# Stick-breaking attention on one core: two heads as one unit, each on its half of the array's rows, and softplus over a whole head

## The chip, the core and the metric

The kernel runs on one core of a Trainium2 chip. The metric is device time in microseconds, from the first to the last instruction of an execution and what lies around it, lower being better. Most executions of a kernel agree within 0.3%.

## What is computed

The kernel is two transformer blocks on 512 tokens of width 1024 in float32. The first has a mixer of stick-breaking attention and a gated linear recurrence (called hgrn in the code), then a mixture of experts; the second has retention, differential attention, attention to a memory and a feed-forward part. The change lies in the stick-breaking attention of the first block: 8 heads of 64 dimensions, 512 queries and keys.

```python
z = einsum('bhqd,bhkd->bhqk', q_blk, k) * dh ** -0.5
mask = key_pos[None, :] < q_pos[:, None]
log_beta = log_sigmoid(z)
log_keep = where(mask, log_sigmoid(-z), 0.0)
later = concatenate([log_keep[..., 1:], zeros_like(log_keep[..., :1])], axis=-1)
log_survive = cumsum(later, axis=3, reverse=True)
a = where(mask, exp(log_beta + log_survive), 0.0)
out = einsum('bhqk,bhkd->bhqd', a, v)
```

With softplus(z) = max(z, 0) + log(1 + exp(-|z|)), log_sigmoid(z) is z - softplus(z) and log_sigmoid(-z) is -softplus(z). So a weight is exp(z minus the sum of softplus over this key and all later ones that the query sees).

## The kernel before

**Products.** A float32 product of the projections is made of three passes over operands split into a rounded part (hi) and the rest (lo): `mm3`, lines 187 to 189. Weights come by DMA in chunks of 128 x 1024 and are split by ScalarE (ACT, L169) and VectorE (DVE, L170). `ws` gives [columns, tokens] by column tiles of 128, 24 products of 512 columns for a tile when the depth is 1024; `ts` gives [tokens, columns]. Their results stand in PSUM under the tag "mm" (2 banks). Attention uses the tag "at" (4 banks) and, for results, "tp" (2 banks).

**Order of the work.** The program is written one operation after the other, and the Tile layer's planner turns it into one fixed order for each engine before the kernel runs: an instruction goes as early as the planner's model has its operands and buffers ready, and of several that are ready the one written first goes first. Work that is written later, such as the gate products behind the attention, thus fills in where the attention would leave an engine idle. Each engine then works in that order and waits on semaphores.

**Slots.** `slot` hands out 128 x 512 tiles of one pool, NSL = 21. The hgrn stage takes 20 of them, 4 of which come free with each of its first three pairs of heads and 8 with the last. Behind them come, in the order of the program, 4 slots for values (`sv_`), 8 for queries (`sq_`), 4 for keys (`sk_`) and 11 of the 16 gates; the other five gates (GX) have a pool of their own, slp2.

**Queries, keys, values.** `ts` makes the values. Then, for each pair t of heads, `ws` makes the pair's queries and keys, 128 rows each, with head 0 on rows 0 to 63 and head 1 on rows 64 to 127. `ev_sq` (L572 to L580) evacuates the queries into a tile of their own for each head, the other head's 64 rows being zeroed by GpSimd (POOL, L578): a product with all 128 rows of the keys then gives that head's scores. The keys are copied as they are (L585).

**A head** (`sb_head`, L605 to L641). Keys lie on partitions. For key block j, only the queries from block j on matter, so that the four blocks have 512, 384, 256 and 128 columns, 1280 in all.

- Scores: for each block a float32 matmul of 128 rows (L615) and a bf16 matmul that adds the mask's -1e30 on the diagonal block (L616, identity times `negsb`). A float32 matmul stands in the profile as two records, its two passes.
- Softplus, block by block: DVE copies the scores to z (L617), ACT takes the absolute value, Exp and Ln (L619 to L621) in one of three buffers "ea", DVE adds max(z, 0) (L622), and `hilo` (L253 on ACT, L254 on DVE) splits the result into ph and pl.
- Sums over later keys: for each block j, products of the triangle or of ones with ph and pl of the blocks from j on (L633, L634), into a bank of "at".
- Weights and values: DVE subtracts the sums from z (L636), ACT takes Exp (L637), and a float32 matmul with 64 columns of the values (L638) writes the head's half of the partitions of y. `hilo` splits y at the end.

z, ph and pl have two buffers each, so a head's can be in use beside the next one's. The scores of the next head take the same four banks "at" as the sums of this one.

**Gates.** Two calls of `ws` behind the heads make 16 tiles; ACT copies each to its slot (L653). Their sigmoids wait for the last Exp of the attention. Then the branch products take the attention's result ysb.

Two other places have matmuls on a half of the array: hgrn's values (L557), where two heads write the two halves of the output partitions, one right behind the other, and differential attention's scores in block 2 (L1182), with 64 rows of each operand and a mask product between one and the next.

Of the kernel before, what the change touches and what calls it, by code (L numbers as in the profile page):

```python
# [8 lines left out]
F32 = mybir.dt.float32  # L9
# [11 lines left out]
S = 512  # L21
# [7 lines left out]
NSL = 21  # L29
GX = (5, 6, 7, 8, 9)  # L30
NRX = 8
NRX2 = 12
# [51 lines left out]
def body(tc, a, out):  # L84
# [106 lines left out]
    def ws(w2, nk, c0, ntile, x, n, evac, lead=0, raws=()):  # L191
        """[cols, tokens] = w2[:, c0:]^T x, by column tiles of 128; `lead` first tiles by halves of the tokens."""
        xh, xl = parts(x)
        per = CE // (nk * 128)
        got = []
        for j in range(ntile):
            if j % per == 0:
                if j // per < len(raws):
                    got = [split(None, nk, per * 128, raws[j // per])]
                else:  # L200
                    got = [load(w2, 0, nk, c0 + j * 128, min(per, ntile - j) * 128)]
            wh, wl = got[0]
            cc = slice((j % per) * 128, (j % per) * 128 + 128)
            if j < lead:
                if j == 0:
                    firsts = []
                o = psum("mm")
                firsts.append((o, wh, wl, cc))
                if j == lead - 1:
                    for hf in range(2):  # L210
                        t0, t1 = hf * n // 2, (hf + 1) * n // 2
                        for o, wh, wl, cc in firsts:
                            for k in range(nk):
                                mm3(o[:, t0:t1], wh[:, k, cc], wl[:, k, cc], xh[k][:, t0:t1], xl[k][:, t0:t1],
                                    k == 0, k == nk - 1)
                    for i, f in enumerate(firsts):
                        evac(i, f[0][:, :n])
                continue
            o = psum("mm")
            for k in range(nk):  # L220
                mm3(o[:, :n], wh[:, k, cc], wl[:, k, cc], xh[k][:, :n], xl[k][:, :n], k == 0, k == nk - 1)
            evac(j, o[:, :n])

    def ts(w2, nk, c0, ntok, x, evac, by_token=True, tag="mm", after=None, korder=None, new=None):
        """[tokens, 512 cols] = x^T w2[:, c0:c0+512]; one block of 128 tokens after the other or all along k."""
# [32 lines left out]
    def normed(xrow, g, p, pre=None):  # L258
        """rmsnorm of 128 rows; `pre`: mean square of the first half, and eps, already summed."""
# [35 lines left out]
    def rms_bcast(m, n, p, w=S, rbufs=2, name="rb"):  # L295
        """1/rms, from sums of squares that stand on every partition."""
        q = p.tile([128, S], F32, name=name, bufs=rbufs)[:, :w]
        A.activation(q, m, AF.Ln, bias=epsc, scale=1.0 / n)
        A.activation(q, q, AF.Exp, scale=-0.5)
        return q  # L300
# [8 lines left out]
    # =====================================================================  # L309
    # block 1, mixer  # L310
    # =====================================================================
# [36 lines left out]
    negsb = cp.tile([128, 128], BF, name="negsb")  # L348
# [17 lines left out]
    # lower bound: first row of the softmax over the two logits  # L366
# [13 lines left out]
    # weights of the differential attention's two maps, and its gains  # L380
# [66 lines left out]
    # cumulative log f inside blocks of 128 tokens; k = 1 - f  # L447
# [26 lines left out]
    def hgrn_pair(t):  # L474
# [43 lines left out]
        # between blocks of 128: the state behind each block, both heads on its diagonal  # L518
# [51 lines left out]
    # stick-breaking attention  # L570
    sq_, sk_, sv_ = {}, {}, {}

    def ev_sq(t0):
        def f(t, o):
            for h in range(2):
                q = slot("sq")
                sq_[2 * (t0 + t) + h] = q
                G.memset(q[64 - 64 * h:128 - 64 * h, :], 0.0)  # L578
                A.activation(q[64 * h:64 * h + 64, :], o[64 * h:64 * h + 64, :], AF.Copy, scale=0.125)
        return f  # L580
# [18 lines left out]
    slp2 = pool("slp2", 1, stack=at)  # L599
# [6 lines left out]
    def sb_head(h):  # L606
        t = h // 2
        z = sb.tile([128, 1280], F32, name="z", bufs=2)
        ph = sb.tile([128, 1280], F32R, name="ph", bufs=2)
        pl = sb.tile([128, 1280], F32R, name="pl", bufs=2)  # L610
        for j in range(4):
            n = S - 128 * j
            cc = slice(COL[j], COL[j + 1])
            o = psum("at")[:, :n]
            T.matmul(o, sk_[t][:, j * 128:(j + 1) * 128], sq_[h][:, j * 128:], start=True, stop=False)  # L615
            T.matmul(o[:, :128], identb, negsb, start=False, stop=True)  # L616
            V.tensor_copy(z[:, cc], o)  # L617
            e = sb.tile([128, S], F32, name="ea", bufs=3)[:, :n]
            A.activation(e, o, AF.Abs)  # L619
            A.activation(e, e, AF.Exp, scale=-1.0)  # L620
            A.activation(e, e, AF.Ln, bias=onec)  # L621
            V.scalar_tensor_tensor(e, z[:, cc], 0.0, e, op0=OP.max, op1=OP.add)  # L622
            hilo(ph[:, cc], pl[:, cc], e)
        y = psum("tp", name="ysbp")
        for j in range(4):
            n = S - 128 * j
            cc = slice(COL[j], COL[j + 1])
            o = psum("at")[:, :n]
            for i in range(j, 4):
                m = tri if i == j else onesr  # L630
                ci = slice(COL[i], COL[i + 1])
                oo = o[:, (i - j) * 128:]
                T.matmul(oo, m, ph[:, ci], start=(i == j), stop=False)  # L633
                T.matmul(oo, m, pl[:, ci], start=False, stop=(i == 3))  # L634
            w = sb.tile([128, S], F32, name="ea", bufs=3)[:, :n]
            V.tensor_sub(w, z[:, cc], o)  # L636
            last_exp[:] = [A.activation(w, w, AF.Exp)]  # L637
            T.matmul(y[64 * (h % 2):64 * (h % 2) + 64, 128 * j:], sv_[j][:, h * 64:(h + 1) * 64], w,  # L638
                     start=(j == 0), stop=(j == 3))
        p0 = 64 * (h % 2)  # L640
        hilo(ysb[0][p0:p0 + 64, t, :], ysb[1][p0:p0 + 64, t, :], y[p0:p0 + 64, :])  # L641

    for h in range(8):
        sb_head(h)

    # gates
    gt = {}

    def ev_gate(key):
        def f(t, o):  # L650
            n = t + (8 if key == "h" else 0)
            gt[key, t] = slot("gt") if n not in GX else slp2.tile([128, S], F32, name="gt2", bufs=len(GX))
# [7 lines left out]
    # branches, output product  # L660
# [40 lines left out]
    def residual_product(w2, xT, p, then, tag="at", korder=None):  # L701
        """x += xT^T w2, the second half of the columns by blocks of tokens; then(t, mean square of the first half)."""
# [13 lines left out]
    # memory rows for the keys and values, and the experts' weights  # L716
# [61 lines left out]
    # =====================================================================  # L778
    # block 1, mixture of experts
    # =====================================================================  # L780
# [6 lines left out]
    def place(v):  # L787
        """per entry of four, how many others stand before it from the greatest down, the earlier of equals first."""
# [32 lines left out]
    # place of a token among its expert's, -1 if it isn't one of them  # L821
# [3 lines left out]
    # weights of the choices  # L825
# [30 lines left out]
    # per token and expert: the token's place, 1, and its weight in three bf16 parts that add up to it  # L856
# [11 lines left out]
    def slots_of(pi, n, ix, w):  # L868
        """row numbers and weights of an expert's slots, from the products with its one-hots."""
# [21 lines left out]
    # experts with more than CAP tokens: how many further blocks  # L891
# [20 lines left out]
    # keys and values of the memory  # L912
# [24 lines left out]
    # rows and outputs of two experts; their transposed rows in both parts  # L937
    XG = hp.tile([128, 4, D], F32, name="XG", tag="hTh")
    XT = hp.tile([128, 4, 8, CAP], F32R, name="XT", tag="hTl")
    def fetch(ix, i):  # L940
        """rows of an expert's slots."""
# [3 lines left out]
    def prep(j, i):  # L945
        """fetched rows, transposed, in both parts."""
# [74 lines left out]
    def load_ahead(e):  # L1021
        """weights that stand ready behind the further blocks, as many as there are buffers."""
# [79 lines left out]
    # values of the memory, behind the experts  # L1102
# [23 lines left out]
    # =====================================================================  # L1126
    # block 2, retention and differential attention
    # =====================================================================
# [186 lines left out]
    # =====================================================================  # L1315
    # block 2, attention to the memory
    # =====================================================================
# [63 lines left out]
    # =====================================================================  # L1381
    # block 2, feed-forward
    # =====================================================================
# [61 lines left out]
```

## Time and profile before

| | |
|---|---|
| median of 3 runs | 1651.45 us |
| lowest to highest | 1650.45 to 1652.04 us |
| span of the profiled execution, first to last instruction | 1649.3 us |
| share of the span: TensorE, DVE, ACT, POOL busy | 98%, 59%, 51%, 5% |

The profiled execution has no time of its own beside its span. Its instructions are given by engine (PE is TensorE's matmuls, PEld its weight loads) and by the line of the code above. A matmul's recorded duration contains the way through the array, so that matmuls which follow each other overlap in the record: what one costs is the distance from its start to the next one's. In a timeline, equal neighbours are merged into one row with their number behind an x. In [ ] stands the idle time of the engine before an instruction and what ended it.

### The profile page before, as it was taken

To read this page: it belongs to the slowest core of one execution; us is meant where nothing else is said; L and a number is where in the kernel's file an instruction comes from. 1 tells how busy PE (TensorE), PEld (TensorE's weight loads), DVE (VectorE), ACT (ScalarE), POOL (GpSimd) and SP (SyncE) were. 2 spreads that over 40 slices of the span, in tenths; PEclk is the share of its full clock that TensorE was granted. 3 is DMA by queue.
4 is the path that set the end of the run, shared out by engine and by line. 5 is a ranking of instruction groups with operands and counts; after the bars stand their busy time and mean duration, and the time that the engine had idled before them with its cause. 6 is when DMAs were issued, how large, how long until landed. Compare 5 with 4: busy or idle time off the path is not lost. (4 is left out here: it accounts for less than half of the span.)

```text
span 1649.3 us, 20584 instructions
## 1 busy us (share of the span) xinstructions
PE 1610.5 (98%) x7695; PEld 1243.8 (75%) x7695; DVE 965.2 (59%) x1541; ACT 837.9 (51%) x1339; POOL 75.1 (5%) x92
## 2 busy tenths in 40 slices
PE   7999999999999999999999999999999999999999
PEld 6887776678878777776677667667878888888887
DVE  6459946544647999998755656455654433333221
ACT  5444556664346888888765545424443423232210
POOL 3000000000001211111110000000000000000000
PEclk9999999999999999999999999999999999999999
DMA  7230220133479999999944113123311333333231
GB/s 229 65 102 26 65 78 26 52 102 98 148 254 301 358 368 365 361 359 374 368 161 141 52 55 86 45 71 114 104 51 51 115 91 101 98 94 103 90 128 39
DMA packets 203071, 242.89 MB, mean 147 GB/s; under 512 B 10400, under 2 KB 133560, under 8 KB 202968
## 3 DMA queue, kind: packets, MB, share of 16 engines
q1 hardware_dynamic: 188800, 205.43, 37.3%
q0 software_dynamic: 7056, 24.27, 5.2%
q10 hardware_dynamic: 7112, 11.85, 2.3%
q8 instruction: 61, 1.00, 0.2%
q14 instruction: 42, 0.34, 0.1%
HBM read 223.69 MB, written 15.73 MB: 145 GB/s over the span
## 5 line engine op out<-in xcount | busy, mean ns | idle before, releaser
L170 DVE TENSOR_TENSOR wlo<-wraw,whi 128x1024 fp32r<-128x1024 f32 x210 | 256.0, 1223 | 280.0 <-ACT whi L169 269.8
L169 ACT CAST whi<-wraw 128x1024 fp32r<-128x1024 f32 x210 | 220.5, 1051 | 380.2 <-PE ps L188 259.8
L187 PE MATMUL ps<-hTh,whi 128*128 128x512 f32 (+1 forms) x912 | 349.7, 384 | 1.3 <-DVE fsg L1396 0.8
L188 PE MATMUL ps<-hTl,whi 128*128 128x512 f32 (+1 forms) x912 | 348.2, 382 | 0.9 <-DVE hTl L254 0.9
L189 PE MATMUL ps<-hTh,wlo 128*128 128x512 f32 (+1 forms) x912 | 347.6, 381 | 0.0
L170 DVE TENSOR_TENSOR wlo<-rx,whi 128x1024 fp32r<-128x1024 f32 x176 | 210.6, 1220 | 36.3 <-ACT whi L169 34.4
L169 ACT CAST whi<-rx 128x1024 fp32r<-128x1024 f32 x176 | 182.8, 1049 | 52.7 <-PE ps L189 30.2
L187 PEld LDWEIGHTS ps<-hTh,whi 128*128 128x128 f32 x912 | 172.1, 189 | 34.6 <-issue 1.8
L188 PEld LDWEIGHTS ps<-hTl,whi 128*128 128x128 f32 x912 | 172.1, 189 | 33.4 <-issue 1.8
L189 PEld LDWEIGHTS ps<-hTh,wlo 128*128 128x128 f32 x912 | 172.1, 189 | 31.8 <-issue 0.9
L187 PE MATMUL ps<-whi,XT 128*96 128x512 f32 x256 | 101.4, 396 | 1.8 <-ACTq L1032 1.8
L189 PE MATMUL ps<-whi,XT 128*96 128x512 f32 x256 | 101.8, 398 | 0.0
L188 PE MATMUL ps<-wlo,XT 128*96 128x512 f32 x256 | 100.8, 394 | 0.0
L189 PE MATMUL ps<-whi,hTl 128*128 128x512 f32 x192 | 77.1, 401 | 0.0
L187 PE MATMUL ps<-whi,hTh 128*128 128x512 f32 x192 | 76.9, 400 | 0.1
L188 PE MATMUL ps<-wlo,hTh 128*128 128x512 f32 x192 | 76.7, 400 | 0.0
L187 PE MATMUL ps<-whi,aTh 128*128 128x512 f32 x176 | 68.5, 389 | 0.0
L188 PE MATMUL ps<-wlo,aTh 128*128 128x512 f32 x176 | 68.5, 389 | 0.0
L189 PE MATMUL ps<-whi,aTl 128*128 128x512 f32 x176 | 68.5, 389 | 0.0
L1396 DVE TENSOR_TENSOR fsg<-fsg,ps 128x512 f32<-128x512 f32 x22 | 15.1, 688 | 76.0 <-PE ps L189 76.0
L187 PEld LDWEIGHTS ps<-whi,XT 128*96 128x96 f32 x256 | 41.3, 162 | 18.5 <-ACTq L1032 2.2
L188 PEld LDWEIGHTS ps<-wlo,XT 128*96 128x96 f32 x256 | 41.4, 162 | 17.3
(458 smaller groups left out, 2677.0 us busy)
## 6 DMA issues: line engine op xcount, KB each, us to landing
wraw<-in_w_in_dram SPq DMA_DIRECT2D x72, 512.0 KB
rx<-in_w_exp_gate_dram SPq DMA_DIRECT2D x58, 512.0 KB
rx<-in_w_exp_down_dram SPq DMA_DIRECT2D x58, 512.0 KB
rx<-in_w_exp_up_dram SPq DMA_DIRECT2D x52, 512.0 KB
wraw<-in_w_gate_dram SPq DMA_DIRECT2D x22, 512.0 KB
wraw<-in_w_up_dram SPq DMA_DIRECT2D x22, 512.0 KB
wraw<-in_w_down_dram SPq DMA_DIRECT2D x22, 512.0 KB
wraw<-in_w_out_dram SPq DMA_DIRECT2D x16, 512.0 KB
```

Of the source, the lines that this page charges most:

```text
L169: i1 = A.copy(hi, w)
L170: i2 = V.tensor_sub(lo, w, hi.bitcast(F32))
L187: T.matmul(o, lh, rh, start=first, stop=False)
L188: T.matmul(o, lh, rl, start=False, stop=False)
L189: T.matmul(o, ll, rh, start=False, stop=last)
L1396: V.tensor_mul(sg[t], sg[t], o)
```

## The change

- Queries are evacuated whole, 128 rows for two heads, without zeros: one ACT instruction for a pair, 4 slots instead of 8.
- `sb_head`, called eight times, becomes `sb_pair`, called four times. Scores of head 0 come from rows 0 to 63 of keys and queries, those of head 1 from rows 64 to 127, one matmul behind the other for each key block.
- The mask is added by DVE while it evacuates the diagonal 128 columns (`negsb` is float32 now); ACT evacuates the other columns. The mask product is gone.
- Absolute value, Exp, Ln, the addition of max(z, 0) and the split run over a head's 1280 columns at once, in a tile e with one buffer. The low part is subtracted by POOL.
- For each key block the sums of both heads, then the values of both heads. The weights are made in place, in z.
- z, ph and pl have 3 buffers (NSB), NSL is 20, and all gates take slots; slp2 and GX are gone.
- Comments and docstrings are removed, line for line.

```diff
-NSL = 21
-GX = (5, 6, 7, 8, 9)
+NSL = 20
 NRX = 8
+NSB = 3
...
-    negsb = cp.tile([128, 128], BF, name="negsb")
+    negsb = cp.tile([128, 128], F32, name="negsb")
...
     def ev_sq(t0):
         def f(t, o):
-            for h in range(2):
-                q = slot("sq")
-                sq_[2 * (t0 + t) + h] = q
-                G.memset(q[64 - 64 * h:128 - 64 * h, :], 0.0)
-                A.activation(q[64 * h:64 * h + 64, :], o[64 * h:64 * h + 64, :], AF.Copy, scale=0.125)
+            sq_[t0 + t] = slot("sq")
+            A.activation(sq_[t0 + t], o, AF.Copy, scale=0.125)
         return f
...
-    slp2 = pool("slp2", 1, stack=at)
...
-    def sb_head(h):
-        t = h // 2
-        z = sb.tile([128, 1280], F32, name="z", bufs=2)
-        ph = sb.tile([128, 1280], F32R, name="ph", bufs=2)
-        pl = sb.tile([128, 1280], F32R, name="pl", bufs=2)
+    def sb_pair(t):
+
+        hs = [slice(64 * h, 64 * h + 64) for h in range(2)]
+        z = [sb.tile([128, 1280], F32, name="z", bufs=NSB) for _ in hs]
+        ph, pl = [], []
         for j in range(4):
             n = S - 128 * j
-            cc = slice(COL[j], COL[j + 1])
-            o = psum("at")[:, :n]
-            T.matmul(o, sk_[t][:, j * 128:(j + 1) * 128], sq_[h][:, j * 128:], start=True, stop=False)
-            T.matmul(o[:, :128], identb, negsb, start=False, stop=True)
-            V.tensor_copy(z[:, cc], o)
-            e = sb.tile([128, S], F32, name="ea", bufs=3)[:, :n]
-            A.activation(e, o, AF.Abs)
+            o = [psum("at")[:, :n] for _ in hs]
+            for h in range(2):
+                T.matmul(o[h], sk_[t][hs[h], j * 128:(j + 1) * 128], sq_[t][hs[h], j * 128:], start=True, stop=True)
+            for h in range(2):
+                zj = z[h][:, COL[j]:COL[j + 1]]
+                V.tensor_add(zj[:, :128], o[h][:, :128], negsb)
+                if n > 128:
+                    A.copy(zj[:, 128:], o[h][:, 128:])
+        for h in range(2):
+            e = sb.tile([128, 1280], F32, name="e", bufs=1)
+            A.activation(e, z[h], AF.Abs)
             A.activation(e, e, AF.Exp, scale=-1.0)
             A.activation(e, e, AF.Ln, bias=onec)
-            V.scalar_tensor_tensor(e, z[:, cc], 0.0, e, op0=OP.max, op1=OP.add)
-            hilo(ph[:, cc], pl[:, cc], e)
+            V.scalar_tensor_tensor(e, z[h], 0.0, e, op0=OP.max, op1=OP.add)
+            ph.append(sb.tile([128, 1280], F32R, name="ph", bufs=NSB))
+            pl.append(sb.tile([128, 1280], F32R, name="pl", bufs=NSB))
+            A.copy(ph[h], e)
+            G.tensor_sub(pl[h], e, ph[h].bitcast(F32))
         y = psum("tp", name="ysbp")
         for j in range(4):
             n = S - 128 * j
...
+            for h in range(2):
+                o = psum("at")[:, :n]
+                for i in range(j, 4):
+                    m = tri if i == j else onesr
+                    ci = slice(COL[i], COL[i + 1])
+                    oo = o[:, (i - j) * 128:]
+                    T.matmul(oo, m, ph[h][:, ci], start=(i == j), stop=False)
+                    T.matmul(oo, m, pl[h][:, ci], start=False, stop=(i == 3))
+                zj = z[h][:, COL[j]:COL[j + 1]]
+                V.tensor_sub(zj, zj, o)
+                last_exp[:] = [A.activation(zj, zj, AF.Exp)]
+            for h in range(2):
+                T.matmul(y[hs[h], 128 * j:], sv_[j][:, (2 * t + h) * 64:(2 * t + h + 1) * 64],
+                         z[h][:, COL[j]:COL[j + 1]], start=(j == 0), stop=(j == 3))
+        hilo(ysb[0][:, t, :], ysb[1][:, t, :], y)
...
-    for h in range(8):
-        sb_head(h)
+    for t in range(4):
+        sb_pair(t)
...
     def ev_gate(key):
         def f(t, o):
-            n = t + (8 if key == "h" else 0)
-            gt[key, t] = slot("gt") if n not in GX else slp2.tile([128, S], F32, name="gt2", bufs=len(GX))
+            gt[key, t] = slot("gt")
             order(A.copy(gt[key, t], o), last_sk[0])
         return f
```

## Rows read from the trace of the kernel before

**Rows 1.** The page: busy time of each engine, and the granted clock in 40 slices.

```profile
span 1649.3 us, 20584 instructions
...
PE 1610.5 (98%) x7695; PEld 1243.8 (75%) x7695; DVE 965.2 (59%) x1541; ACT 837.9 (51%) x1339; POOL 75.1 (5%) x92
...
PEclk9999999999999999999999999999999999999999
```

**Rows 2.** Busy time by stretch, columns in the first line, x counts instructions.

```profile
core 0: us, PE busy (x) PEld busy (x) DVE busy (x) ACT busy (x) POOL busy (x), PEclk, DMA share, GB/s
210.20:231.70 21.50, 21.50 (x95) 17.62 (x94) 6.14 (x7) 7.89 (x12) 0.00 (x0) 1.00 0.34 98
231.70:358.30 126.60, 123.58 (x561) 83.99 (x559) 73.66 (x145) 85.03 (x189) 0.00 (x0) 1.00 0.14 42
358.30:391.30 33.00, 33.00 (x147) 27.31 (x147) 8.04 (x7) 17.25 (x28) 0.00 (x0) 1.00 0.48 159
```

**Rows 3.** Groups of ACT, 231.7 to 358.3: xcount, busy us, mean ns, idle before.

```profile
L169 ACT CAST whi<-wraw 128x1024 fp32r<-128x1024 f32 x10 | 10.5, 1045 | 4.7 <-PE ps L188 4.5
...
L653 ACT COPY gt<-ps 128x512 f32<-128x512 f32 x9 | 5.2, 579 | 0.0
```

**Rows 4.** Timeline of TensorE (start us, us), 231.5 to 234.4, first head.

```profile
231.71 1.02 PE L615 MATMUL ps<-sq,sk 128*128 128x512 f32 x2
232.56 0.22 PE L616 MATMUL ps<-negsb,identb 128*128 128x128 bf16 x1
...
234.22 0.47 PE L187 MATMUL ps<-hTh,whi 128*128 128x512 f32 x1
```

**Rows 5.** Timeline of TensorE, 244.5 to 249.7: second scores, first values.

```profile
244.78 1.10 PE L615 MATMUL ps<-sq,sk 128*128 128x512 f32 x2 [0.25 <-DVE ea L636]
245.81 2.37 PE L638 MATMUL ysbp<-ea,sv 128*64 128x512 f32 x8
248.11 0.23 PE L616 MATMUL ps<-negsb,identb 128*128 128x128 bf16 x1
```

**Rows 6.** Timeline of TensorE, 338 to 339.6, the start of the last head.

```profile
338.51 1.10 PE L615 MATMUL ps<-sq,sk 128*128 128x512 f32 x2 [0.31 <-DVE ea L636]
```

**Rows 7.** Timeline of TensorE, 915 to 919, 64-row matmuls of block 2.

```profile
915.45 0.52 PE L1197 MATMUL ps<-ident,pp 128*128 128x128 f32 x3
915.89 1.12 PE L1182 MATMUL ps<-dk,dq 64*128 64x512 f32 x2
916.95 0.94 PE L1201 MATMUL ps<-aT,dv 128*128 128x128 f32 x6
```

**Rows 8.** Timeline of TensorE, hgrn stage; last, line L557 (ns min/median/max).

```profile
106.23 1.95 PE L481 MATMUL ps<-hq,hk 128*128 128x128 f32 x16
...
123.97 0.44 PE L557 MATMUL ps<-std,hv 128*64 128x128 f32 x4
...
L557 PE MATMUL ps<-std,hv x64: 272/298/324, 124.0 to 208.5; 128*64 128x128 f32 x64
```

**Rows 9.** Groups by form, ACT and DVE, 231.7 to 358.3: busy us, mean ns.

```profile
L621 ACT ACTIVATE ea<-ea,onec 128x512 f32<-128x512 f32 x8 | 5.7, 717 | 0.0
...
L620 ACT ACTIVATE ea<-ea 128x512 f32<-128x512 f32 x8 | 5.1, 633 | 0.1
...
L253 ACT CAST ph<-ea 128x512 fp32r<-128x512 f32 x8 | 5.0, 620 | 0.0
...
L620 ACT ACTIVATE ea<-ea 128x128 f32<-128x128 f32 x8 | 2.5, 309 | 0.1
...
L622 DVE SCALAR_TENSOR_TENSOR ea<-z,ea 128x512 f32<-128x512 f32 x8 | 5.5, 693 | 8.4 <-ACT ea L621 8.4
...
L622 DVE SCALAR_TENSOR_TENSOR ea<-z,ea 128x128 f32<-128x128 f32 x8 | 2.3, 287 | 0.8 <-ACT ea L621 0.7
```

**Rows 10.** Groups of POOL, 400 to 470.

```profile
L747 POOL MEMSET hn<- 128x1024 f32 x1 | 1.0, 959 | 234.4 <-issue 234.4
```

**Rows 11.** The line that evacuates values: ns min/median/max, first and last start.

```profile
L590 ACT COPY sv<-ps x4: 562/587/587, 119.8 to 162.1; 128x512 f32<-128x512 f32 x4
```

More of the change, by code (lines that the diff above doesn't have):

```diff
@@ L626, in sb_head @@
             n = S - 128 * j
[L627 to L641, printed above, removed]
-    for h in range(8):
-        sb_head(h)
+            for h in range(2):
[15 more added lines that the diff above has]
+        sb_pair(t)
     gt = {}
```

## The prediction

> **What bounds the kernel now.** I read the page's busy table and clock line first: TensorE is busy for 1610.5 us, 98% of a span of 1649.3 us, at a granted clock of 9 tenths or more in every slice [rows 1]. So the question is how much TensorE time the attention takes, and whether the new form leaves TensorE standing.
>
> Next come the busy times by stretch [rows 2]. From 210.2 to 231.7 us TensorE runs projections alone. From 231.7 to 358.3 us the eight heads run, with TensorE recorded busy for 123.6 of 126.6 us, DVE for 73.7 and ACT for 85.0: only TensorE is full. From 358.3 to 391.3 us it does nothing but gate products. The gates are the filling: 24 products each, and 9 of the 16 were evacuated while the heads ran [rows 2, 3]. Six gates in 33.0 us make 5.5 us each, 88 us for 16. Of the 159.6 us from 231.7 to 391.3, the rest, 71.6 us, belongs to the heads.
>
> Then the TensorE timeline. The first head's scores, undisturbed, start at 231.71 and a gate product follows at 234.22: 2.51 us with the four mask products, or 20.1 us for eight heads [rows 4]. A head's eight value records run from 245.81 to 248.11, 2.30 us, 18.4 us in all [rows 5]. What remains of the 71.6, 33.1 us, is the sums over later keys (not changed) and standstills.
>
> The last thing to see is the order. Heads follow each other at the pace of a chain: head 2's scores start at 244.78, head 8's at 338.51, so a head takes 15.6 us, and each start is released by a subtraction (L636) of the head before, which frees a bank of its sums [rows 5, 6], while from 234.22 on, with its score banks being drained, TensorE did gates instead of starting head 2. I read that as the score banks being handed out in program order. That decides what can stand next to what in the new order.
>
> **Scores.** The 32 mask products go, and a head's matmul uses 64 rows. The nearest rows are block 2's 64-row matmuls: two passes of 512 columns take 915.89 to 916.95, 0.53 us each, where two passes on 128 rows take 0.85 (231.71 to 232.56), 0.43 each [rows 4, 7]. So a pass on half the rows is 0.10 us dearer, not cheaper. With 0.107 us less for each 128 columns fewer, a head costs 2 x (0.533 + 0.427 + 0.320 + 0.213) = 2.99 us. One after the other, eight heads cost 23.9, 3.8 more than now. The gain has to come from two heads running at once. No row shows that for row halves. For column halves one does: four records of hgrn's values, two heads of two passes, end after 0.44 us though each lasts 0.30; sixteen records on the full array are 0.11 apart (1.95 us), and four at that spacing would take 0.61 [rows 8]. I take it that row halves overlap as well, but only where both heads' matmuls stand next to each other. If all did, four pairs cost 12.0, 8.1 less. The lower end is thus -8.1, the upper +3.8. By the bank order I expect later pairs to start with one score block alone, as each head does now at 244.78 with the values behind it [rows 5], and the remaining seven to overlap: 1.07 + 2.99 = 4.06 a pair, 2.99 for the first. That is 15.2, and some 1.6 for changes of shape (three transposes from 915.45, 0.11 apart, are through at 915.78 and the 64-row pass starts at 915.89 [rows 7]: 0.10, twice around each of two clusters in four pairs): 16.8, or **-3.3 us**.
>
> The Trainium skill, "TensorEngine Tiling (Array Packing)", Theoretical Speedup, gives up to 2x for a dimension of 64 or less, for rows as for columns. By that alone the scores would fall from 20.1 to 10 us.
>
> **Values.** The two heads already write the two column halves, but eight records of one head stand together now. If both heads overlapped throughout, 18.4 would become about 9.5 (two passes of 0.43 for 512 columns, so 2.15 a pair, and some 0.2 for weight loads between passes and shape changes): -8.9. Overlap needs both heads' weights ready together. They aren't: the new tile e has one buffer, so the second head's softplus starts when the first head's low part is done, and the first head's values, next in order, go alone long before. I expect a quarter of the ideal, **-2 us**; +1 if each block stands alone between gates, with two changes of shape of 0.10 each.
>
> **The chain.** From the rows of 512 and 128 columns, carried on to 1280 (Exp's 0.84 ns a column for all of ACT): Exp 1.28, the absolute value as much, Ln 1.36, copy 1.27; the DVE step 1.51 at 1.06 ns a column [rows 9]. The subtraction for the low part goes to POOL, which did no arithmetic here. Its nearest row is the memset, 0.96 us for 1024 columns [rows 10], 1.2 for 1280; two inputs and an output at that pace would be 3.6. I take 2.4, between them, as two inputs have to be read. A head's softplus is then 9.1 us, with hand-overs 9.7, two heads in turn 19.4. With 4.5 for scores and draining (ACT now copies some 1.2 us of them per head), 1.7 for the last sums and subtraction, and gate work in ACT's queue (1.05 and 0.58 us a gate [rows 3], two or three gates), a pair takes some 29 us where two heads took 31.2. Four pairs end near 352, with 5 gates left. POOL's time thus costs nothing while gates last; they last until the chain exceeds 33.1 + 16.8 + 16.4 + 88 = 154 us, 38 a pair.
>
> The Trainium skill's "GPSIMD Engine Reference", Elementwise, has 4497 ns for a two-input add of 2048 columns; scaled, that is an estimate of 2.8 us here, which no run yet shows, and a pair would last 30 us.
>
> **Small edits.** DVE loses the whole-width copies and the low parts; it has 53 us of slack in the stretch [rows 2]: nothing. The query evacuation becomes one ACT instruction instead of two and a POOL memset: hidden by 210.2 to 231.7, where ACT is busy for 7.9 us. One slot fewer holds up the first value evacuation, at 119.8 us [rows 11], until the first hgrn pair frees its four; the two product banks take two tiles meanwhile, 48 products or 11 us: nothing, or 1 us. Gates now wait for slots: 8 are free and each pair frees two: nothing while a pair uses 3. Standstills I leave alone, with 3 us either way: TensorE's recorded idle is 3.0 us [rows 2].
>
> **Sum.** -3.3 - 2.0 = -5.3 us. The profiled span is 1649.3 us; the median of the runs, 1651.45, stands 2.15 above it, and that margin stays. 1649.3 - 5.3 + 2.15 = 1646.2.
>
> **Rivals.**
> - Both overlap fully: -8.1 - 8.9 = -17, 1634.5. For it: the two column halves do overlap [rows 8]. Against: the single e buffer and the bank order. The 2x of the Trainium skill's "TensorEngine Tiling (Array Packing)" would be this case.
> - Slower: row halves don't overlap. Place: the score matmuls. Price: +3.8 for the 64-row passes [rows 7], 1.6 for shape changes, with values gaining nothing: 1651.45 + 5.4 = 1656.9. It decides if the second head's first pass doesn't start before the first head's second has ended. Against it: the column halves.
> - TensorE stands at the low parts: the order is fixed, and where POOL is later than planned, each head's first low-part product waits. At 1.5 us a head, 12 us less the 5.3: 1658. For it: POOL has no arithmetic row. The Trainium skill's "SBUF — State Buffer", Who interferes with whom, says a DVE instruction with two SBUF inputs and a POOL instruction that reads SBUF exclude each other; here that would be a gate's low part on DVE ahead of POOL's. No row shows it.
> - The change doesn't do what it says: the planner spreads the pairs so that nothing overlaps beyond the loss of the mask products: about 1651.
>
> **Chances.** About 0.2% (3.3 us) is what a measurement can tell. Forecast 0.45, of which 0.38 faster; full overlap 0.17; no row overlap 0.16, 0.12 of it slower; TensorE waiting for POOL 0.08, slower; nothing gained 0.14, 0.03 of it faster. Faster 0.58, within 0.22, slower 0.20. The range takes in full overlap and most of the no-overlap case: 1634 to 1656.
>
> **What would show it.** Scores: two heads' records at one start, and later pairs' first block alone. Values: the first head's records well before the second's. POOL: eight subtractions of 1.2 to 3.6 us. Chain: a pair's start every 26 to 32 us, last values near 350, then about 5 gates alone. I am wrong if the values stand in pairs (faster than 1640), if the 64-row passes keep 0.53 us spacing with one head after the other, or if TensorE's idle exceeds 8 us between 231 and 360.

## The result, and the profile after

The changed kernel takes 1661.49 us (median of 4 runs, 1660.10 to 1662.88) beside 1651.74 for the kernel before on the same chip (4 runs, 1650.45 to 1652.08): 1.0058 of its time, 95% interval 1.0045 to 1.0071. It is slower by 9.75 us, where 5.3 us less was forecast. The profiled execution took 1660.1 us, its span is 1658.3.

The page of the kernel after (span, busy time, clock) answers to [rows 1]:

```profile
span 1658.3 us, 20321 instructions
...
PE 1605.6 (97%) x7663; PEld 1239.5 (75%) x7663; DVE 945.2 (57%) x1481; ACT 829.7 (50%) x1259; POOL 93.9 (6%) x92
...
PEclk9999999999999999999999999999999999999999
```

TensorE is busy for 4.9 us less and the span is 9.0 us longer: the time went into TensorE standing. The windows of the kernel after (columns as in [rows 2]) say where:

```profile
210.20:231.70 21.50, 21.50 (x96) 17.35 (x95) 6.08 (x7) 7.17 (x10) 0.00 (x0) 1.00 0.30 88
231.70:358.30 126.60, 111.60 (x496) 77.15 (x494) 49.95 (x79) 76.84 (x106) 22.10 (x8) 0.99 0.15 44
358.30:400.00 41.70, 40.24 (x182) 31.24 (x183) 12.11 (x14) 20.42 (x35) 1.18 (x1) 1.00 0.39 127
```

In the heads' stretch TensorE does nothing for 15.0 us, where it was 3.0 before. DVE and ACT are busy for less of it than before (49.95 and 76.84 us, from 73.7 and 85.0); POOL is busy for 22.1 us, from none. The stage, from the first head's scores to the first branch product, lasts from 232.55 to 399.99, 167.44 us, beside 159.56 before (231.71 to 391.27). That is +7.9; the stage begins 0.8 us later, and behind it the kernels take 1258.3 and 1258.0 us.

The waits of TensorE in the stage name the cause. Columns: engine, tile and line that waited, what it waited for, us in total, times, longest. The kernel after:

```profile
PE ps L637 <- POOL pl L626: 13.2, 8, 1.8
PE ps L611 <- ACT z L616: 2.5, 4, 1.2
PE ysbp L642 <- ACT z L640: 0.8, 3, 0.3
```

and the kernel before:

```profile
PE ysbp L638 <- ACT ea L637: 1.5, 3, 0.5
PE ps L615 <- DVE ea L636: 1.3, 5, 0.3
```

Eight waits, one in each head, for POOL's low part: 13.2 us. The timeline of the kernel after shows the first of them (start us, us):

```profile
244.79 0.47 PE L636 MATMUL ps<-ph,tri 128*128 128x512 f32 x1
...
244.85 2.90 POOL L626 TENSOR_TENSOR pl<-e,ph 128x1280 fp32r<-128x1280 f32 x1 [210.03 <-ACT ph L625]
...
245.79 0.39 PE L188 MATMUL ps<-hTl,whi 128*128 128x512 f32 x1
247.78 1.28 ACT L619 ACTIVATE e<-z 128x1280 f32<-128x1280 f32 x1 [2.60 <-POOL pl L626]
...
247.81 0.50 PE L637 MATMUL ps<-pl,tri 128*128 128x512 f32 x1 [1.62 <-POOL pl L626]
```

The high part is ready, and TensorE starts the first sum with it (L636); POOL starts the subtraction 0.06 us later. In TensorE's order four gate products follow, the last at 245.79, and then the first product with the low part (L637). POOL needs 2.90 us, so it comes at 247.81. There are gate products left to do, 5.8 gates of them when the last value product has run at 368.37, but they stand behind L637. The second head's softplus waits as well: it needs the one tile e, which POOL is still reading (L619 at 247.78).

The rest of the change did what it was for. A sum for each kind of matmul over the stage, from each record's start to the next record's start (so that a standstill counts with the record ahead of it), in us:

| | scores with mask | gates | high sums | low sums | values | stage |
|---|---|---|---|---|---|---|
| before | 22.0 | 92.5 | 12.7 | 12.6 | 19.8 | 159.6 |
| after | 17.2 | 96.5 | 18.5 | 16.3 | 18.9 | 167.4 |

Scores gave 4.8 and values 0.9. Gates and sums, whose products the change does not touch, cost 13.6 more: they hold the standstills.

### The profile page after: what moved, and what is told of

Read it like the earlier page. It is cut to its first block, busy times and chain, and to the rows that moved or that the text cites. A ratio compares the mean times of both kernels' runs of the same rounds, so it can differ in the third digit from the quotient of the medians.

```text
span 1658.3 us, 20321 instructions
## 1 busy us (share of the span) xinstructions
PE 1605.6 (97%) x7663; PEld 1239.5 (75%) x7663; DVE 945.2 (57%) x1481; ACT 829.7 (50%) x1259; POOL 93.9 (6%) x92
## 5 line engine op out<-in xcount | busy, mean ns | idle before, releaser
L170 DVE TENSOR_TENSOR wlo<-wraw,whi 128x1024 fp32r<-128x1024 f32 x210 | 261.8, 1251 | 286.0 <-ACT whi L169 277.5
L187 PEld LDWEIGHTS ps<-whi,XT 128*96 128x96 f32 x256 | 41.7, 163 | 18.8 <-ACTq L1034 2.2
L189 PEld LDWEIGHTS ps<-whi,XT 128*96 128x96 f32 x256 | 41.8, 163 | 17.3
```

The lines of the kernel that those rows point to most:

```text
L170: i2 = V.tensor_sub(lo, w, hi.bitcast(F32))
L187: T.matmul(o, lh, rh, start=first, stop=False)
L189: T.matmul(o, ll, rh, start=False, stop=last)
```

## The experiments

The theory after this result: TensorE's order was fixed for a low part that comes soon, POOL takes longer, and that is the whole loss. The rivals: the chain of a pair is too long whichever engine subtracts (one e buffer, five instructions in a row over 1280 columns), or the scores' start in pairs costs it. For each run the table has the median, the ratio to the kernel before beside it, and the sums of one profiled execution as above.

| run | median us | ratio, 95% interval | scores | gates | high | low | values | stage |
|---|---|---|---|---|---|---|---|---|
| e1 | 1645.87 | 0.9953, 0.9936 to 0.9969 | 17.2 | 89.9 | 12.7 | 13.8 | 17.0 | 150.6 |
| e2 | 1662.42 | 1.0067, 1.0050 to 1.0084 | 22.0 | 92.1 | 20.2 | 15.5 | 19.4 | 169.2 |
| e3 | 1644.51 | 0.9952, 0.9936 to 0.9969 | 18.7 | 89.9 | 12.6 | 13.9 | 17.0 | 152.1 |
| e4 | 1635.53 | 0.9898, 0.9882 to 0.9915 | 14.9 | 89.5 | 10.6 | 12.4 | 13.2 | 140.7 |
| e5 | 1630.87 | 0.9865, 0.9849 to 0.9882 | 15.0 | 91.7 | 11.0 | 13.4 | 9.2 | 140.4 |
| e6 | 1638.35 | 0.9914, 0.9898 to 0.9931 | 18.3 | 89.7 | 10.8 | 12.1 | 13.2 | 144.1 |
| e7 | 1672.88 | 1.0123, 1.0106 to 1.0140 | 17.2 | 94.8 | 25.8 | 18.1 | 21.9 | 177.7 |
| e8 | 1640.69 | 0.9930, 0.9910 to 0.9950 | 17.7 | 90.2 | 11.6 | 14.3 | 13.2 | 147.0 |
| e9 | 1638.86 | 0.9914, 0.9900 to 0.9927 | 17.8 | 92.3 | 10.9 | 13.8 | 9.2 | 144.0 |
| e10 | 1647.57 | 0.9971, 0.9958 to 0.9984 | 15.0 | 96.7 | 19.3 | 14.6 | 9.2 | 154.9 |

### e1: the low part on DVE

```diff
-            G.tensor_sub(pl[h], e, ph[h].bitcast(F32))
+            V.tensor_sub(pl[h], e, ph[h].bitcast(F32))
```

> The changed kernel with the low part subtracted by DVE instead of POOL, nothing else. Theory (TensorE stands at each head's first low-part product because POOL takes 2.9 us where the fixed order left it about 1): the eight waits, 13.2 us, go, and with them the falls of the clock that follow them, some 3 us: 1644 to 1649 us. Rival (softplus over a whole head makes the chain too long: a pair's start every 34 us where two heads took 31.2): the pace changes by the 2.9 to 1.5 us a head at most and the time stays above 1655 us.

One word changes the time from 1661.49 to 1645.87 us, 15.6 less, and puts the kernel ahead of the one before. The timeline of e1, at the same place of the first head:

```profile
245.60 1.49 DVE L626 TENSOR_TENSOR pl<-e,ph 128x1280 fp32r<-128x1280 f32 x1
...
245.64 0.47 PE L636 MATMUL ps<-ph,tri 128*128 128x512 f32 x1
...
247.14 0.51 PE L637 MATMUL ps<-pl,tri 128*128 128x512 f32 x1
```

The subtraction takes 1.49 us, and TensorE fills it with gate products without standing; its waits in this stage hold no low part at all. Pairs start 29.2, 30.0 and 29.0 us apart (233.43, 262.62, 292.66, 321.70), where the changed kernel had 33.7 (a third of the way from 232.55 to 333.70). The rival that the chain is too long whichever engine subtracts falls. The planner's order differs too: between a head's first high and first low product it put five to eight products (1.2 to 1.7 us) for DVE's 1.49 us, but only four to six (0.9 to 1.3 us) for POOL's 2.9. What its model holds for POOL is not on record.

### e2: the kernel before, with its low parts on POOL

```diff
-            hilo(ph[:, cc], pl[:, cc], e)
+            A.copy(ph[:, cc], e)
+            G.tensor_sub(pl[:, cc], e, ph[:, cc].bitcast(F32))
```

> The kernel before with the low part of each block subtracted by POOL, nothing else. Theory (POOL later than the order expects): TensorE waits for POOL in each of the eight heads, at least 1 us a head, 8 us or more: 1660 us or more. Rival (POOL is harmless, whole-head softplus is the cost): 1650 to 1654 us.

The opposite test, on the old layout, with no pairs and three buffers for the softplus: 10.4 us slower than the kernel before, as the theory had it. The waits of e2:

```profile
PE ps L635 <- POOL pl L624: 7.5, 20, 0.5
```

Here too TensorE waits at the low parts, in shorter pieces (7.5 us, a little under the 8 us expected). So the loss needs neither the pairs nor the one buffer e: POOL's subtraction alone brings it.

### e3: e1 with the scores of one head after the other

```diff
-        for j in range(4):
-            n = S - 128 * j
-            o = [psum("at")[:, :n] for _ in hs]
-            for h in range(2):
-                T.matmul(o[h], sk_[t][hs[h], j * 128:(j + 1) * 128], sq_[t][hs[h], j * 128:], start=True, stop=True)
-            for h in range(2):
+        for h in range(2):
+            for j in range(4):
+                n = S - 128 * j
+                o = psum("at")[:, :n]
+                T.matmul(o, sk_[t][hs[h], j * 128:(j + 1) * 128], sq_[t][hs[h], j * 128:], start=True, stop=True)
...
```

> As e1_low_on_dve, but the scores of head 0 are written first, all four blocks, and then those of head 1, so that neighbours stand on the same half of the rows. Theory (the overlap of the row halves is worth its price): scores go from 4.3 us a pair to 2 x 2.99 and shape changes, about 6.3: 8 us more than e1. Rival (the overlap is worth little, since gates fill in anyway): within 2 us of e1.

The two heads' row halves no longer stand next to each other, and nothing is lost: 1644.51 beside 1645.87 us, with overlapping ranges (1642.54 to 1646.58, 1641.14 to 1647.26). The theory here fell. The timeline of TensorE shows why, in e3:

```profile
232.58 2.42 PE L611 MATMUL ps<-sq,sk 64*128 64x512 f32 x8
234.93 0.50 PE L187 MATMUL ps<-hTh,whi 128*128 128x512 f32 x1
```

and in the kernel after:

```profile
232.55 1.77 PE L611 MATMUL ps<-sq,sk 64*128 64x512 f32 x8
235.56 1.42 PE L611 MATMUL ps<-sq,sk 64*128 64x256 f32 x8 [1.23 <-ACT z L616]
236.91 0.50 PE L187 MATMUL ps<-hTh,whi 128*128 128x512 f32 x1
```

A head alone costs 2.35 us, two 4.70: its 64-row passes follow each other closely. In pairs the first sixteen records cost 4.36 us, and 1.23 of these are a standstill. Two heads with 8 blocks need 8 banks and the tag "at" has 4, so that the third block's scores wait until ACT has drained the first ones. In e3 gate products (from 234.93) stand where the pair stands still.

### e4: e1 with a pair's value products behind all its sums

```diff
                 last_exp[:] = [A.activation(zj, zj, AF.Exp)]
+        for j in range(4):
             for h in range(2):
                 T.matmul(y[hs[h], 128 * j:], sv_[j][:, (2 * t + h) * 64:(2 * t + h + 1) * 64],
```

> As e1_low_on_dve, but the value matmuls of a pair are written behind all its sums, head 0 and head 1 in turn for each block. Theory (column halves overlap once neighbours stand on different halves): values go from some 4.5 us a pair to 2.5: 6 to 9 us less than e1. Rival (they were hidden, or wait for the last Exp instead): within 2 us of e1.

10.3 us less than e1, somewhat more than the 6 to 9 of the theory. The timeline of TensorE in e4:

```profile
258.94 2.37 PE L643 MATMUL ysbp<-z,sv 128*64 128x512 f32 x14
261.23 1.77 PE L611 MATMUL ps<-sq,sk 64*128 64x512 f32 x8
```

Fourteen of a pair's sixteen value records take 2.29 us, where one head's eight took 2.30 before [rows 5]: both column halves work at once when their products stand next to each other and are ready together. But the values gave only 3.8 of the stage's some 10 us (17.0 to 13.2, some 3.3 a pair where 2.5 was expected, since one head's first block still stands alone). Sums and scores gain too (10.6, 12.4 and 14.9 us, from 12.7, 13.8 and 17.2): a later pair's scores now start with eight records together, as at 261.23, where e1 has one block of one head in front. For the sums I take it that this is because no single value products of another shape stand between them, which was not tried by itself.

### e5: e4 with two buffers e

```diff
-            e = sb.tile([128, 1280], F32, name="e", bufs=1)
+            e = sb.tile([128, 1280], F32, name="e", bufs=2)
...
-            ph.append(sb.tile([128, 1280], F32R, name="ph", bufs=NSB))
+            ph.append(sb.tile([128, 1280], F32R, name="ph", bufs=2))
```

> As e4_values_together, with two buffers for e (and two instead of three for ph, for room). Theory (TensorE's own work is the bound, the chain is covered by gates): the second head's softplus no longer waits for the first's low part, a pair's pace falls from 27.5 to some 24 us, and the time stays within 2 us of e4. Rival (the chain still sets the end): 4 us or more below e4.

1630.87 us, the fastest of all and 21.5 less than the kernel before beside it (1652.32). All sixteen value records now stand together, 9.2 us for the kernel. By the medians the theory missed: 4.7 us below e4 is what the rival asked for. The rival's reason isn't what the trace shows, though: at the last value product 8.6 gates are left (5.9 in e4), so the chain is covered, and what fell is TensorE's own work, 4.0 us of values, which the theory had left as it was. The stage of the profiled execution is no shorter than e4's, but that execution was the slowest of the four (1637.12; the others 1628.26 to 1631.57). It has a granted clock of 0.992, the others 0.997 or 0.998. The windows of e5 (columns as in [rows 2]) show a place where the clock falls:

```profile
262.00:266.00 4.00, 4.00 (x19) 3.34 (x18) 0.26 (x1) 4.00 (x5) 0.00 (x0) 1.00 0.44 131
266.00:268.70 2.70, 0.53 (x4) 0.11 (x2) 1.81 (x2) 2.70 (x4) 0.00 (x0) 1.00 0.00 0
268.70:272.10 3.40, 3.40 (x8) 2.75 (x9) 3.25 (x3) 3.40 (x4) 0.00 (x0) 0.50 0.02 5
```

TensorE stands for 2.17 us, for a gate's evacuation on ACT, and then runs at half clock (1.2 GHz) for 3.4 us. The two cost up to 3.9 us of this stage; the faster executions have no trace.

### e6: e3 and e4 together

The diffs of e3 and e4, both on the kernel after, with the low part on DVE.

> As e4_values_together, with the scores written head by head as in e3_scores_by_head. Theory (the overlap of the row halves brings no more than the 1.5 us of TensorE time between e1 and e3, as the four banks must be drained in between): 0 to 3 us above e4. Rival (with the values out of the way the overlap is worth its full price, two heads of 2.35 us against one): 6 us or more above e4.

2.8 us slower than e4, within what the theory had: once the values stand together, writing the scores in pairs is worth a little (14.9 us of scores beside 18.3).

### e7: the change, with POOL's subtraction in four pieces

```diff
-            G.tensor_sub(pl[h], e, ph[h].bitcast(F32))
+            for j in range(4):
+                cc = slice(COL[j], COL[j + 1])
+                G.tensor_sub(pl[h][:, cc], e[:, cc], ph[h][:, cc].bitcast(F32))
```

> The changed kernel with the low part still on POOL, but in four instructions of 512, 384, 256 and 128 columns. Theory (what TensorE waits for is the time from POOL's start to the first block that the first low-part product reads): the first waits shrink to under 1 us a head, in all 4 to 9 us instead of 13.2, and the time lies at 1652 to 1658 us. Rival (POOL's whole time decides, whatever the pieces): as the changed kernel, 1660 us or more.

Neither account holds: it is 11.4 us slower than the kernel after. The first waits of the heads did shrink to at most 0.7 us, as the theory had it, but others came behind them, and the time lies far above its range. The waits of TensorE in e7:

```profile
PE ps L639 <- POOL pl L628: 10.6, 18, 1.1
```

The groups of POOL in e7 (xcount, busy us, mean ns, idle before):

```profile
L628 POOL TENSOR_TENSOR pl<-e,ph 128x512 fp32r<-128x512 f32 x8 | 10.2, 1280 | 303.5 <-ACT ph L625 303.5
L628 POOL TENSOR_TENSOR pl<-e,ph 128x256 fp32r<-128x256 f32 x8 | 8.8, 1097 | 0.0
L628 POOL TENSOR_TENSOR pl<-e,ph 128x384 fp32r<-128x384 f32 x8 | 8.0, 1004 | 0.0
L628 POOL TENSOR_TENSOR pl<-e,ph 128x128 fp32r<-128x128 f32 x8 | 4.6, 577 | 0.0
```

The same group in the kernel after:

```profile
L626 POOL TENSOR_TENSOR pl<-e,ph 128x1280 fp32r<-128x1280 f32 x8 | 23.3, 2910 | 301.4 <-ACT ph L625 301.4
```

The pieces take 31.6 us where whole heads took 23.3, a head 3.96 instead of 2.91 us, and TensorE waits 18 times instead of 8. The means hide two cases. The timelines of POOL and DVE in e7:

```profile
247.54 0.72 POOL L628 TENSOR_TENSOR pl<-e,ph 128x256 fp32r<-128x256 f32 x1
...
281.70 2.08 DVE L170 TENSOR_TENSOR wlo<-wraw,whi 128x1024 fp32r<-128x1024 f32 x1 [2.62 <-ACT whi L169]
...
282.67 1.70 POOL L628 TENSOR_TENSOR pl<-e,ph 128x256 fp32r<-128x256 f32 x1
```

With no gate's low part on DVE beside them, the four pieces take 1.27, 1.00, 0.72 and 0.45 us, 3.4 in all. In four heads one piece took 1.0 us longer (three of 256 columns, 1.70 or 1.71 us, one of 128, 1.44), each while such a low part was under way on DVE. The planner also put only one or two products between the first high and the first low product. The clock fell to half four times in this stage, where it did once in the kernel after: some 5 us of the stage's 10.3 more (three more times 3.4 us at half). What makes the rest stays open.

### e8: e4 with softplus block by block

```diff
+            for j in range(4):
+                cc = slice(COL[j], COL[j + 1])
+                e = sb.tile([128, S], F32, name="ea", bufs=2)[:, :S - 128 * j]
+                A.activation(e, z[h][:, cc], AF.Abs)
...
+                hilo(ph[h][:, cc], pl[h][:, cc], e)
```

> As e4_values_together, with absolute value, Exp, Ln, addition and split by key block (two buffers of 512 columns) instead of over a whole head. Theory (softplus is off the path as long as gates cover it, whatever its grain): within 3 us of e4. Rival (the grain counts, by the longer chain of whole heads): 5 us or more below e4.

5.2 us slower than e4, where the theory had within 3 us and the rival 5 us or more faster: both missed. So softplus over a whole head is no loss here; it helps. The difference lies in the scores (+2.7 us) and the sums (+2.9); why they grow was not tried.

### e9: e5 with DVE draining the score banks

```diff
                 if n > 128:
-                    A.copy(zj[:, 128:], o[h][:, 128:])
+                    V.tensor_copy(zj[:, 128:], o[h][:, 128:])
```

> As e5_two_e_buffers, with all columns of the scores evacuated by DVE, none by ACT. Theory (the scores of a pair stand still in the middle because their four banks wait for ACT's copies, 1.7 us in the first pair and 0.9 in the others, 2.4 us of recorded waits in e4): the waits for ACT go, and 1 to 3 us with them: 1628 to 1631 us. Rival (DVE drains no sooner): within 1 us of e5 in the stage's length, with waits for DVE in the place of those for ACT.

The waits of e9:

```profile
PE ps L611 <- DVE z L616: 2.7, 4, 1.2
```

The scores' wait for the drain is as long as it was with ACT (2.6 us in e5), only on DVE, as the rival had it: DVE drains no sooner. But the kernel is 8.0 us slower than e5, and the stage 3.5, where the rival had within 1 us. 2.8 us of that are scores, whose last blocks now stand in part between gate products; what makes the rest stays open.

### e10: e5 with the low part on POOL again

```diff
-            V.tensor_sub(pl[h], e, ph[h].bitcast(F32))
+            G.tensor_sub(pl[h], e, ph[h].bitcast(F32))
```

> As e5_two_e_buffers, with the low part on POOL again. Theory (the order is fixed before the run and leaves POOL some 1 us of its 2.9, whatever stands around it): TensorE waits for POOL in each head again, 10 us or more in all, and the time lies 10 to 18 us above e5. Rival (in a shorter chain with values at the end POOL has the slack): within 4 us of e5.

16.7 us slower than e5, with the waits of e10:

```profile
PE ps L637 <- POOL pl L626: 12.7, 8, 2.1
```

With two buffers e, values together and shorter stages, POOL costs as much as it did in the change (15.6 us between e1 and the kernel after). A second buffer doesn't cover it: the planner put one to five products ahead of the low part's, no more than in the change. POOL is also slower here. The timelines of POOL and DVE in e10:

```profile
247.42 3.17 DVE L170 TENSOR_TENSOR wlo<-wraw,whi 128x1024 fp32r<-128x1024 f32 x1 [0.95 <-ACT whi L169]
...
249.46 3.89 POOL L626 TENSOR_TENSOR pl<-e,ph 128x1280 fp32r<-128x1280 f32 x1
```

In three of the four pairs the second head's subtraction takes 3.88 or 3.89 us, with a gate's low part on DVE under way when it starts.

## Why the prediction was wrong

**The step that failed** is "The chain", in its sentence that POOL's time costs nothing while gates last. Gates lasted: 5.8 were left at the end, as before (6.0), and the forecast had 5. But a gate product can cover a wait only where it stands ahead of the waiting product in TensorE's order, and that order is made before the kernel runs. Between the first head's first high and first low product stood some 1.2 us of work (from 244.79 to 0.23 us, the distance of two gate products, behind 245.79), 0.9 to 1.3 in the other heads, and POOL needed 2.9. The eight waits came to 13.2 us, and the idle time of the stretch to 15.0, beyond the 8 us that the prediction had set as a sign of being wrong. The step named a cover and never looked at whether the cover stands in the right place. It should have been priced as the rival had it: POOL's duration less what the planner leaves, times eight heads, since each head has its own first low part.

**POOL's duration** was a lesser miss. I took 2.4 us between 1.2 and 3.6, and it was 2.90 to 2.92. At 2.4, TensorE would by the same order still have stood for 1.1 us a head (0.5 less than 1.6), 9 us in all. The Trainium skill's "GPSIMD Engine Reference", Elementwise, scaled to 2.8 us: the trace agrees with it, 2.91 us.

**The rival "TensorE stands at the low parts"** is what happened, with a price close to the measured one: 1.5 us a head and 12 us in all beside 1.65 and 13.2; its 1658 us beside 1661.49. I gave it 0.08 although the missing row on POOL's arithmetic stood there as an argument for it.

**The port.** The Trainium skill's "SBUF — State Buffer", Who interferes with whom, has DVE instructions with two SBUF inputs and POOL's reads of SBUF exclude each other. The trace agrees (2.76 us for a low part that takes 1.22 elsewhere), but in the kernel after it was the other way round from the rival: not a gate's low part ahead of POOL's, but DVE held up by POOL. The timeline of the kernel after, POOL and DVE:

```profile
279.62 2.91 POOL L626 TENSOR_TENSOR pl<-e,ph 128x1280 fp32r<-128x1280 f32 x1 [21.45 <-ACT ph L625]
...
280.85 2.76 DVE L170 TENSOR_TENSOR wlo<-wraw,whi 128x1024 fp32r<-128x1024 f32 x1 [2.61 <-ACT whi L169]
```

That low part ended at 283.61, 1.08 us after POOL did (282.53), as if nearly all of its 1.22 us had been done only then. Four of the sixteen in the stage, at 280.85, 291.60, 347.23 and 357.95, took 2.60 to 2.76 us. Behind each DVE waited again, for TensorE's sums (0.27 us at 283.88), and POOL's own eight lasted 2.90 to 2.92 us with or without them: here the lock lengthened what had time to spare. The rival's own case is in e7 and e10, where POOL's subtraction took 1.0 us longer behind a gate's low part.

**Scores.** The cost was near, 17.2 us where 16.8 was forecast; the gain was 4.8 instead of 3.3, since the scores had cost 22.0 before and not eight times the undisturbed first head, 20.1. Its terms were off both ways. Passes on 64 rows that follow each other are cheaper than the two of block 2 which stand alone between other shapes [rows 7]: a head's eight take 2.35 us in e3 where I had 2.99. And row halves overlap, as I took it from the column halves [rows 8], from the first pair on. But the overlap is worth only some 1.5 us over the kernel (17.2 in e1, 18.7 in e3), because of the wait for the banks, 2.5 us in all. The prediction had drawn a lone first block from the order of the banks, and it came; the timeline of TensorE in the kernel after, second pair:

```profile
266.85 1.12 PE L611 MATMUL ps<-sq,sk 64*128 64x512 f32 x2
267.90 0.44 PE L642 MATMUL ysbp<-z,sv 128*64 128x128 f32 x4
268.27 1.86 PE L611 MATMUL ps<-sq,sk 64*128 64x512 f32 x8
270.54 1.04 PE L611 MATMUL ps<-sq,sk 64*128 64x256 f32 x6 [0.41 <-ACT z L616]
```

What it had not seen is the standstill in the middle, 1.23 us in the first pair and 0.41 in the others. The cheaper passes, which no row had shown, made up for it: that the cost came out so near is luck in part.

**Values.** 0.9 us less in the change, 2.8 without POOL (17.0 in e1), where 2 was forecast. Of the two reasons given, the program's order weighs more than the single buffer e: e4, still with one buffer, has fourteen of sixteen records together, and the second buffer (e5) adds the last two. Together they show the part of the ideal that was withheld, 19.8 to 9.2 us, near the 9.5 forecast.

**The chain's pace** of 29 us a pair was right without POOL: 29.4 in e1. With POOL it was 33.7.

**The sum.** -5.3 us was forecast, and e1, the change without POOL's arithmetic, has -6.1 beside its own kernel before (1645.87 and 1651.99). So of the forecast's 15.3 us of error (1661.49 less 1646.2) POOL's subtraction is 15.6. That the rest adds up is luck in part: in the profiled execution of e1 the stage is 8.9 us shorter than before (150.64 beside 159.56), its first scores come 1.7 us later, and behind the stage 3.4 us are lost. The hgrn stage gave the first scores of the kernel after 0.8 us later, as "nothing, or 1 us" had it. That was not separately tried.

**The clock.** The fall to half clock was not in the forecast. The windows of the kernel after (columns as in [rows 2]), around the second standstill:

```profile
256.00:258.20 2.20, 0.38 (x4) 0.23 (x2) 0.00 (x0) 0.00 (x0) 2.16 (x1) 1.00 0.81 233
258.20:259.70 1.50, 1.48 (x10) 1.44 (x11) 0.19 (x1) 0.00 (x0) 0.00 (x0) 1.00 0.01 3
259.70:263.10 3.40, 3.40 (x10) 1.66 (x8) 1.51 (x3) 1.57 (x3) 0.00 (x0) 0.51 0.00 0
```

At half clock 3.4 us do the work of 1.7, so this one fall costs up to 1.7 us. Two of the four runs have a mean clock of 0.993 and take 1662.62 and 1662.88 us; the other two, at 0.997 and 0.995, take 1660.10 and 1660.37.

## What to carry to other kernels

Where an order is fixed before the kernel runs, spare work covers a slower instruction only if it stands ahead of the waiting one in that order, so for a step moved to another engine compare its duration there with the distance between its producer and its first reader. Whether POOL's subtraction can be hidden by more spare work ahead of the waiting product was not tried. Matmuls on half of the array pay when two that use different halves are written next to each other and are ready together: writing the values so was worth 10 us (e4), 3.8 of them in the values themselves, and for the scores it was worth little, since the banks ran out midway. The version to keep is e5: the change with the low part on DVE, the values of a pair together, and two buffers e.

## What the runs showed of the hardware that was not expected

- POOL's subtraction of two operands over 128 x 1280 takes 2.91 us where DVE takes 1.49 (e1), and cutting it up is dear: 1.27, 1.00, 0.72 and 0.45 us for 512, 384, 256 and 128 columns when left alone (e7), 3.4 in all. A gate's low part under way on DVE adds 1.0 us (e7, e10).
- TensorE's granted clock fell to half for 3.4 us behind standstills: at 259.7 in the kernel after (TensorE stood from 256.4 to 258.2) and at 268.7 in e5 (2.17 us). Their length alone doesn't decide it: seven of the kernel after's eight waits for POOL, of 1.56 to 1.71 us, were followed by no fall, and e7's four falls followed standstills of at most 1.1 us. What does decide it was not tried.
- A float32 pass on 64 rows and 512 columns takes 0.53 us only at the head of its run, 0.43 behind it (first two records of e3 at 232.58); 0.43 is the distance of full-array passes [rows 4].
